# Hybrid attention and MoE layer, one core: the last four experts combined one by one on TensorE's row strips, with the sums and the residual kept in PSUM

## The chip, the cores and the metric

The kernel runs on one core of a Trainium2 chip. The metric is the device time of one execution in microseconds (us), as the median of several runs; lower is better. Engines are named as in the profile: PE is TensorE, PEld its weight loads, DVE VectorE, ACT ScalarE, POOL GpSimd, SP the engine that issues nearly all transfers.

## The reference

One decoder layer on 256 tokens of width 1024, in float32. Two groups of attention heads share one input projection; their outputs go through one output projection and are added to the residual. The part that matters here is the channel mixer behind it, a mixture of 32 experts, of which each token uses two:

```python
def hier_moe(h, ...):                  # h = rms_norm(x): 256 tokens x 1024
    g = argmax(t @ router_group)       # one of 4 groups of experts
    top_v, top_e = top_k(e_logits, 2)  # two of the 8 experts in it
    weight = p_group * softmax(top_v)
    ...
    hid = silu(xc @ w_gate[e]) * (xc @ w_up[e])      # 1024 -> 256
    return hid @ w_down[e]                           # 256 -> 1024
    ...
    y = zeros.at[slot_tok].add(out * slot_w)
x = x + y
```

The weights of each expert are three matrices of 1 MB, and all 32 experts are read in every execution: 96 MB of the 122 MB that are read.

## The kernel before

**Stages.** The first third of the time is attention; the rest is a loop over the experts `e = 1 .. 31` (L854 to L877), in groups of `G = 4`. Each expert has room for `CAP = 32` tokens, so the four experts of a group fill 128 rows. Weights come as units of 1 MB through a ring of buffers (`fill`, L117); SP issues them in the order of `units`: gate and up of an expert, then down of the expert two before it. The last two units are the down weights of experts 30 and 31; the very last one is issued in pieces of columns, `CUTS`.

**One expert.** `half` (L635) multiplies the gathered tokens by gate or up weights: eight matmuls with 32 output rows each, placed side by side in four column strips of the array (`tile_position=(0, q * CAP)`), so that four run at a time. `gate` and `up` copy the result out of PSUM (ScalarE at L650, VectorE at L655). `folded` (L657) transposes it in four pieces on TensorE, then VectorE sums (L663, L665), ScalarE applies silu and VectorE multiplies (L667): the result is `hT`. `down` (L675) multiplies `hT` by the down weights, again in four column strips, and copies the four strips into rows of one tile per group, `oG` (`oL` for the last group), by turns on ScalarE (L686) and VectorE (L688).

**One group.** `weighted` (L616) turns the routing weights of a group into a matrix `pT` (tokens by slots): VectorE multiplies the two 0/1 matrices `P` by the weights `W` into the buffers `Ps`, TensorE transposes them, ScalarE copies. `combine` (L699) then multiplies `pT` by the group's outputs and accumulates over the groups in four PSUM banks `y`. It runs in the third expert of the next group. After the seventh group `combined` adds `y` to the residual `x2` on VectorE (L697).

**The end.** `last` (L706) does the down product of expert 31 in five column slices. For each slice: two matmuls in one column strip (L714), a ScalarE copy (L716), two matmuls with the `pT` of the last group (L726), two VectorE adds to `x2` (L727), an output transfer on SP (L728). `warmed` (L670) runs matmuls on zeros as fillers.

**What sets the order.** `pe` (L632) pins TensorE's instructions to the order of the program. The other engines' queues are ordered by a scheduler. PSUM tiles share eight banks through tags (`lg`, `av`, `pp`, `tr`, two each); a tile waits until the tile before the last with its tag was read.

"Down product of expert 30" in this text is the group of eight matmuls that `down` issues for it; in TensorE's timeline it starts at 328.54.

Of the kernel before, what the change touches and what calls it, by code (L numbers as in the profile page):

```python
# [20 lines left out]
P = 128  # L21
S = 256
# [13 lines left out]
CUTS = (0,256,512,768,896,1024)  # L36
# [14 lines left out]
def hybrid_layer_kernel(ctx: ExitStack, tc: tile.TileContext, x, xt, w_in, w_out, w_gate, w_up, w_down, smalls, relb, out):  # L51
# [65 lines left out]
    def fill(i, limit=len(units)):  # L117
        while len(tiles) < limit:
            j = len(tiles)
            h = home(j)  # L120
            if h not in pools:
                return
            cap = size[h] - (3 if h == "ring" and over_at - RING <= i < over_at else 0)
            if len(used[h]) >= cap and used[h][len(used[h]) - cap] >= i:
                return
            src, k, parts = units[j]
            t = pools[h].tile([P, 2048], F32, name=f"u{j}", tag=h)
            tv = t.rearrange("p (k f) -> p k f", k=k)
            for q in range(parts):
                if j == 0:  # L130
                    ks = slice(q * k // parts, (q + 1) * k // parts)
                    nc.sync.dma_start(tv[:, ks], src[:, ks])
                    xt_load(2, 4) if q == 0 else xt_load(4, 8)
                elif j < len(units) - 1:
                    nc.sync.dma_start(tv, src)
                else:
                    for a, b in zip(CUTS, CUTS[1:]):
                        nc.sync.dma_start(tv[:, :, a:b], src[:, :, a:b])
            tiles.append(t)
            used[h].append(j)  # L140
# [444 lines left out]
    G = 4  # L585
    x2p = x2.rearrange("t c (p k) -> t c k p", k=KC)
# [28 lines left out]

    def weighted(st):  # L616
        g = st["g"]
        pt = ps.tile([P, 512], F32, name="ptr", tag="tr")
# [5 lines left out]
        if g < E // G - 1:  # L624
            st["pT"] = ex.tile([P, S], F32, name="pT", tag="pT")
            st["o"] = ex.tile([P, D], F32, name="oG", tag="oG")
        else:
            t = pools["late"].tile([P, 2048], F32, name="oL", tag="late")
            st["o"], st["pT"] = t[:, :D], t[:, D : D + S]
# [44 lines left out]

    def down(e, st, hT, low):  # L675
        j0 = (e % G) * CAP
        dv = unit(place[e][2], low).rearrange("p (c n) -> p c n", c=2)
        pd = ps.tile([P, 512], F32, name="pd", tag="tr")
        for c in range(2):
            for j in range(4):  # L680
                pe(nc.tensor.matmul(pd[j * 32 : (j + 1) * 32, :256], hT[:, c, :], dv[:, c, j * 256 : (j + 1) * 256],  # L681
                                    start=c == 0, stop=c == 1, tile_position=(0, j * 32)))
        for j in range(4):
            dst = st["o"][j0 : j0 + CAP, j * 256 : (j + 1) * 256]
# [7 lines left out]
    def combined(st, c, nh):  # L692
        pe(nc.tensor.matmul(y[c][nh], st["pT"][:, c * P : (c + 1) * P], st["o"][:, nh * 512 : (nh + 1) * 512],  # L693
                            start=st["g"] == 0, stop=st["g"] == E // G - 2))
        if st["g"] == E // G - 2:
            dst = x2[:, c, nh * 512 : (nh + 1) * 512]
            nc.vector.tensor_tensor(dst, dst, y[c][nh], op=ALU.add)  # L697

    def combine(st):  # L699
        if not y:  # L700
            y.extend([ps.tile([P, 512], F32, name="y", tag=t) for t in ("lg", "av")] for _ in range(NC))
        for c in range(NC):
            for nh in range(2):
                combined(st, c, nh)

    def last(e, st, hT):  # L706
        j0 = (e % G) * CAP
        dv = unit(place[e][2]).rearrange("p (c n) -> p c n", c=2)

        def first(j):  # L710
            pd = ps.tile([P, 512], F32, name="pd", tag="pp")
            a, b = CUTS[j], CUTS[j + 1]
            for c in range(2):
                pe(nc.tensor.matmul(pd[j0 : j0 + CAP, : b - a], hT[:, c, :], dv[:, c, a:b],  # L714
                                    start=c == 0, stop=c == 1, tile_position=(0, j0)))
            nc.scalar.activation(st["o"][j0 : j0 + CAP, a:b], pd[j0 : j0 + CAP, : b - a], AF.Copy)  # L716

        first(0)
        for j in range(len(CUTS) - 1):
            if j < len(CUTS) - 2:  # L720
                first(j + 1)
            cs = slice(CUTS[j], CUTS[j + 1])
            w = CUTS[j + 1] - CUTS[j]
            for c in range(NC):
                py = ps.tile([P, 512], F32, name="py", tag="lg" if c == 0 else "av")
                pe(nc.tensor.matmul(py[:, :w], st["pT"][:, c * P : (c + 1) * P], st["o"][:, cs], start=True, stop=True))  # L726
                nc.vector.tensor_tensor(x2[:, c, cs], x2[:, c, cs], py[:, :w], op=ALU.add)  # L727
            nc.sync.dma_start(out[:, cs].rearrange("(c p) n -> p c n", p=P), x2[:, :, cs])  # L728
# [125 lines left out]
    for e in range(1, E):  # L854
# [13 lines left out]
        if e == E - 1:  # L868
            warmed(2, "lg")
# [4 lines left out]
    hT = folded(t)  # L874
    down(*queue.pop(0), place[E - 1][0])
    warmed(2, "lg")
# [75 lines left out]
```

## Time and profile before

| | us |
|---|---|
| median of three runs (342.51 to 344.88) | 344.61 |
| the profiled execution | 344.07 |
| its span, first to last instruction | 342.2 |

The times in the rows below are those of the profiled execution, counted from the start of its span; its own time is 1.9 us more than the span. The page gives TensorE 314.2 us of busy time, 92% of the span, VectorE 198.9, ScalarE 140.1. Transfers moved 123.17 MB, at 360 GB/s over the span. A busy TensorE in such a page is not one at its peak: records of matmuls that run side by side overlap, and the time of a group is read from where it starts to where the next one starts.

### The profile page before, as it was taken

What the parts mean: (1) busy time and instruction counts of PE and PEld (TensorE: products, weight loads), DVE (VectorE), ACT (ScalarE), POOL (GpSimd) and SP (SyncE); (2) the same over time, 40 slices, a digit from 0 to 9 for tenths busy, and PEclk for the clock granted to TensorE, in tenths of its full rate; (3) what the DMA queues carried; (4) which work ended last, traced back from release to release, by engine and by line L of the source; (5) the groups of instructions that cost most, each with busy time, mean ns of one, the idle gap of its engine ahead of it and who ended that gap; (6) DMA issues with size and microseconds to landing.
All of it is one profiled execution on the core that took longest, in us unless ns stands there. A gap on an engine that the chain in (4) does not pass through costs nothing.

```text
span 342.2 us, 7096 instructions
## 1 busy us (share of the span) xinstructions
PE 314.2 (92%) x2685; PEld 204.8 (60%) x2685; DVE 198.9 (58%) x604; ACT 140.1 (41%) x363; POOL 13.3 (4%) x21
## 2 busy tenths in 40 slices
PE   6999999999999998999999999999678769958875
PEld 2758876788777788575564755646234524724333
DVE  1759758887999657756364563636233521534533
ACT  4775677868786434324222242322112121222221
POOL 1100001000120131000000000000000000000000
PEclk9999999999999999999999999999699988998999
DMA  6999999999625896599999999999999999999953
GB/s 195 398 385 291 389 387 400 412 411 417 215 67 210 313 422 252 205 415 415 417 415 419 415 416 418 416 411 417 417 419 418 416 417 415 411 419 414 410 175 123
DMA packets 31206, 123.17 MB, mean 360 GB/s; under 512 B 2343, under 2 KB 5972, under 8 KB 22980
## 3 DMA queue, kind: packets, MB, share of 16 engines
q1 hardware_dynamic: 30868, 121.70, 90.1%
q0 software_dynamic: 304, 1.02, 0.9%
q8 instruction: 22, 0.36, 0.4%
q14 instruction: 12, 0.10, 0.1%
HBM read 121.64 MB, written 1.07 MB: 359 GB/s over the span
## 4 chain that ended last, share of the span: by engine, by line
PE 63%; DMA 31%; DVE 3%; ACT 1%; issue 0%; SPq 0%; DVEq 0%
PE pp L251 26%; DMA u<-in_w_gate_dram 12%; DMA u<-in_w_down_dram 12%; PE pgu L643 10%; DMA u<-in_w_up_dram 6%; PE pd L681 5%; PE pg L611 4%; PE y L693 3%; PE ptr L660 3%; PE lg L310 2%; DMA u<-in_w_in_dram 2%; PE pt L337 1%; PE pd L714 1%; PE py L726 1%; PE pt L286 1%; PE at L358 1%
## 5 line engine op out<-in xcount | busy, mean ns | idle before, releaser
L643 PE MATMUL pgu<-u,xe 128*32 128x256 f32 x1024 | 71.6, 399 | 10.9 <-ACT oG L686 4.8
L251 PE MATMUL pp<-hi,xh 128*128 128x512 f32 (+1 forms) x132 | 54.1, 411 | 2.4 <-ACT hi L240 2.4
L643 PEld LDWEIGHTS pgu<-u,xe 128*32 128x32 f32 x1024 | 31.1, 112 | 41.2 <-issue 10.9
L251 PE MATMUL pp<-hi,xl 128*128 128x512 f32 (+1 forms) x132 | 52.6, 399 | 0.0
L686 ACT ACTIVATE oG<-pd 32x256 f32<-32x256 f32 x56 | 20.9, 374 | 76.8 <-PE pd L681 63.2
L251 PE MATMUL pp<-lo,xh 128*128 128x512 f32 (+1 forms) x132 | 52.2, 400 | 0.1
L241 DVE TENSOR_TENSOR lo<-u,hi 128x512 fp32r<-128x512 f32 x62 | 43.2, 713 | 13.4 <-ACT hi L240 13.0
L240 ACT ACTIVATE hi<-u 128x512 fp32r<-128x512 f32 x64 | 39.1, 627 | 18.9 <-PE pp L251 13.0
L688 DVE COPY oG<-pd 32x256 f32<-32x256 f32 x56 | 23.7, 423 | 39.5 <-ACT oG L686 37.6
L681 PE MATMUL pd<-u,hT 128*32 128x256 f32 x496 | 34.7, 398 | 8.7 <-DMA u<-in_w_down_dram 7.0
L251 PEld LDWEIGHTS pp<-hi,xh 128*128 128x128 f32 x132 | 25.5, 194 | 9.9 <-ACT hi L240 4.1
L251 PEld LDWEIGHTS pp<-lo,xh 128*128 128x128 f32 x132 | 25.5, 193 | 6.9 <-issue 1.0
L251 PEld LDWEIGHTS pp<-hi,xl 128*128 128x128 f32 x132 | 25.6, 194 | 4.7
L655 DVE COPY u<-pgu 128x256 f32<-128x256 f32 x32 | 13.5, 423 | 24.6 <-PE pgu L643 24.6
L681 PEld LDWEIGHTS pd<-u,hT 128*32 128x32 f32 x496 | 14.8, 112 | 21.2 <-issue 6.7
L611 PEld LDWEIGHTS pg<-Ps,x2q 128*128 128x128 f32 x224 | 25.5, 192 | 2.9 <-DVE gu L663 2.5
L611 PE MATMUL pg<-Ps,x2q 128*128 128x128 f32 x224 | 26.9, 278 | 0.0
L693 PE MATMUL y<-oG,pT 128*128 128x512 f32 x56 | 25.9, 605 | 0.0
L660 PEld LDWEIGHTS ptr<-sm,u 128*128 128x128 f32 x128 | 14.3, 148 | 14.3 <-issue 11.8
L660 PE MATMUL ptr<-sm,u 128*128 128x128 f32 x128 | 22.4, 300 | 0.0
L663 DVE TENSOR_REDUCE gu<-ptr 128x64 f32<-128x256 f32 x32 | 13.6, 425 | 13.2 <-PE ptr L660 12.4
L650 ACT ACTIVATE u<-pgu 128x256 f32<-128x256 f32 x32 | 12.3, 383 | 14.0 <-PE pgu L643 13.4
(155 smaller groups left out, 327.7 us busy)
## 6 DMA issues: line engine op xcount, KB each, us to landing
u<-in_w_gate_dram SPq DMA_DIRECT2D x32, 1024.0 KB, 20.0
u<-in_w_up_dram SPq DMA_DIRECT2D x32, 1024.0 KB, 19.9
u<-in_w_down_dram SPq DMA_DIRECT2D x31, 1024.0 KB, 20.0
u<-in_w_in_dram SPq DMA_DIRECT2D x11, 1024.0 KB, 12.4
u<-in_w_out_dram SPq DMA_DIRECT2D x4, 1024.0 KB, 14.6
u<-in_w_in_dram SPq DMA_DIRECT2D x2, 512.0 KB, 6.1
x<-in_x_dram SPq DMA_DIRECT2D x2, 512.0 KB, 11.1
bias<-rdr SPq DMA_DIRECT2D x3, 256.0 KB, 4.6
```

The lines of the kernel that those rows point to most:

```text
L240: nc.scalar.activation(hi, raw, AF.Copy)
L241: (nc.gpsimd if u * 4 + k in (0,3,) else nc.vector).tensor_tensor(lo, raw, hi.bitcast(F32), op=ALU.subtract)
L251: yield lambda a=a, w=w, kk=kk, i=i: nc.tensor.matmul(pp, a, w[:, cols], start=first and kk == 0 and i == 0, stop=last and kk == len(hls) ...
L611: pe(nc.tensor.matmul(pg[:, j * P : (j + 1) * P], x2q[:, c, q4 * 4 + j, :], st["P"][c][1], start=c == 0, stop=c == NC - 1))
L643: pe(nc.tensor.matmul(pg[q * CAP : (q + 1) * CAP, :HID], st["xe"][:, k, j0 : j0 + CAP], wv[:, k, :], start=r == 0, stop=r == KC // ROWS_Q ...
L655: nc.vector.tensor_copy(t[:, HID : 2 * HID], pg[:, :HID])
L660: pe(nc.tensor.transpose(pt[:, j * P : (j + 1) * P], t[:, j * P : (j + 1) * P], ident))
L663: nc.vector.tensor_reduce(gu[:, :2], parts[:, :2], axis=AX.X, op=ALU.add)
L681: pe(nc.tensor.matmul(pd[j * 32 : (j + 1) * 32, :256], hT[:, c, :], dv[:, c, j * 256 : (j + 1) * 256], start=c == 0, stop=c == 1, tile_pos ...
L686: nc.scalar.activation(dst, pd[j * 32 : (j + 1) * 32, :256], AF.Copy)
L688: nc.vector.tensor_copy(dst, pd[j * 32 : (j + 1) * 32, :256])
L693: pe(nc.tensor.matmul(y[c][nh], st["pT"][:, c * P : (c + 1) * P], st["o"][:, nh * 512 : (nh + 1) * 512], start=st["g"] == 0, stop=st["g"] ...
```

## The change

The last group (experts 28 to 31) is no longer combined as a whole.

- `weighted_last` makes a `pT` for each of its four experts. The expert's 32 weighted columns are repeated four times, so that after the transpose they stand on all four blocks of 32 rows. This is four pairs of VectorE products and transposes, and four ScalarE copies, where there was one of each pair.
- `down` of these experts leaves the result as it lies in PSUM: block `j` of 32 rows holds columns `256 j` to `256 j + 255`. `moved` copies it out, 128 columns by ScalarE and 128 by VectorE, instead of four copies of strips.
- `spread` adds one expert to `y`: for each `j` and each half `c` of the tokens a matmul on the 32 rows of block `j`, in row strip `j` of the array (`tile_position=(j * CAP, 0)`), into bank `y[j]`. The banks are now split by columns (four of 256), with both halves of the tokens in each.
- The residual is added in PSUM too: `residual` multiplies `x2` by the identity, four matmuls of 256 columns for each half of the tokens. The four adds of L697 and the ten of L727 are gone.
- In the last unit (down weights of expert 31) the pieces are now the first 128 of 256 rows whole, then the other 128 in two halves of columns. `last` does the product of the first rows, two fillers, and then each half: product, move, sums, copies from `y` to `x2`, and one output transfer from each of two queues, ScalarE's and SP's.
- In TensorE's order `folded` of expert 31 moves ahead of the down product of expert 29; the residual's matmuls stand behind the down products of 28 and 29, the sums of experts 28 and 29 ahead of the down product of 30.

```diff
-CUTS = (0,256,512,768,896,1024)
+CUTS = ((0, 0, 1024), (1, 0, 512), (1, 512, 1024))
...
+    CROSS = [(j, c) for c in range(NC) for j in range(4)]
...
+    def weighted_last(st):
+        t = pools["late"].tile([P, 2048], F32, name="oL", tag="late")
+        st["o"], st["pT"] = t[:, :D].rearrange("p (i n) -> p i n", i=G), t[:, D:].rearrange("p (i t) -> p i t", i=G)
+        for i in range(G):
+            pt = ps.tile([P, 512], F32, name="ptr", tag="tr")
+            for c in range(NC):
+                q = st["P"][c][1].rearrange("p (j s) -> p j s", j=G)
+                e = st["g"] * G + i
+                nc.vector.tensor_scalar(q, st["P"][c][0][:, i : i + 1, :].broadcast_to([P, G, CAP]),
+                                        W[:, c, e : e + 1], None, op0=ALU.mult)
+                pe(nc.tensor.transpose(pt[:, c * P : (c + 1) * P], q.rearrange("p j s -> p (j s)"), ident))
+            nc.scalar.activation(st["pT"][:, i, :], pt[:, :S], AF.Copy)
...
+    def moved(st, i, pd, rows):
+        nc.scalar.activation(st["o"][rows, i, :P], pd[rows, :P], AF.Copy)
+        nc.vector.tensor_copy(st["o"][rows, i, P:], pd[rows, P:256])
+
+    def spread(st, i, pairs):
+        for j, c in pairs:
+            r = slice(j * CAP, (j + 1) * CAP)
+            pe(nc.tensor.matmul(y[j][:, c * 256 : c * 256 + 256], st["pT"][r, i, c * P : (c + 1) * P],
+                                st["o"][r, i, :], start=False, stop=i == G - 1 and c == NC - 1, tile_position=(j * CAP, 0)))
...
+    def residual(c):
+        for j in range(4):
+            pe(nc.tensor.matmul(y[j][:, c * 256 : c * 256 + 256], ident, x2[:, c, j * 256 : (j + 1) * 256],
+                                start=False, stop=False))
...
     def last(e, st, hT):
...
+        down_product(hT, dv, pd, (0,), range(4))
+        warmed(2, "pp")
+        for nh in range(2):
+            down_product(hT, dv, pd, (1,), (2 * nh, 2 * nh + 1))
+            moved(st, G - 1, pd, slice(nh * 64, nh * 64 + 64))
+            j0 = 2 * nh
+            spread(st, G - 1, [(j, c) for c in range(NC) for j in (j0, j0 + 1)])
+            for c, eng in enumerate((nc.scalar, nc.sync)):
+                for j in (j0, j0 + 1):
+                    dst = x2[:, c, j * 256 : (j + 1) * 256]
+                    if j == j0:
+                        nc.scalar.activation(dst, y[j][:, c * 256 : c * 256 + 256], AF.Copy)
+                    else:
+                        nc.vector.tensor_copy(dst, y[j][:, c * 256 : c * 256 + 256])
+                eng.dma_start(out[c * P : (c + 1) * P, nh * 512 : nh * 512 + 512], x2[:, c, nh * 512 : nh * 512 + 512])
...
         if e == E - 1:
-            warmed(2, "lg")
+            hT = folded(t)
         if e > 1:
             down(*queue.pop(0), place[e][0])
         if e == OVER_E:
             overflow()
-    hT = folded(t)
+        if e == E - 2:
+            residual(0)
+    residual(1)
+    spread(st, 0, CROSS)
+    spread(st, 1, CROSS)
     down(*queue.pop(0), place[E - 1][0])
-    warmed(2, "lg")
+    spread(st, 2, CROSS)
     last(E - 1, st, hT)
```

The order of the built programs shows what this moves. In these rows the names are those of the tiles, `sm` holds the identity, `x_64` is `x2`, numbers belong to units of weights, and brackets name the engines or transfer queues (DMAHW) whose signals an instruction waits for. First, TensorE behind the up product of expert 30. Before:

```order
L623 MATMUL ptr<-sm,Ps 128x128 x2
L681 MATMUL pd<-u_3204,hT 32x256 [waits DMAHW0_49,DVE_49,PE_49]
L681 MATMUL pd<-u_3204,hT 32x256 x7
L643 MATMUL pgu<-u_3206,xe 32x256 [waits DMAHW1_49,Activation_49]
L643 MATMUL pgu<-u_3206,xe 32x256 x7
```

Now:

```order
L627 MATMUL ptr<-sm,Ps 128x128 x2
L627 MATMUL ptr<-sm,Ps 128x128 [waits DVE_49] x2
L627 MATMUL ptr<-sm,Ps 128x128 [waits DVE_49,Activation_49]
L627 MATMUL ptr<-sm,Ps 128x128 [waits DVE_49]
L627 MATMUL ptr<-sm,Ps 128x128 [waits DVE_49,Activation_49]
L627 MATMUL ptr<-sm,Ps 128x128 [waits DVE_49]
L690 MATMUL pd<-u_3224,hT 32x256 [waits DMAHW0_49,Activation_49]
L690 MATMUL pd<-u_3224,hT 32x256 x7
L730 MATMUL y<-x_64,sm 128x256 x4
L655 MATMUL pgu<-u_3226,xe 32x256 [waits DMAHW1_49]
```

One pair of transposes became four, six of them with a wait for VectorE, and four residual matmuls (L730) stand ahead of the gate product of expert 31. VectorE at the same place, before:

```order
L697 TENSOR_TENSOR x_64<-x_64,y 128x512 [waits PE_49,Pool_49]
L655 COPY u_3083<-pgu 128x256 [waits DMAHW6_49,PE_49]
L688 COPY oL<-pd 32x256 [waits Activation_49] x2
L663 TENSOR_REDUCE gu<-ptr 128x64 [waits DVE_49,PE_49]
L665 TENSOR_REDUCE gu<-ptr 128x64
L655 COPY u_3206<-pgu 128x256 [waits DMAHW1_49,PE_49]
```

Now:

```order
L667 COPY u_3103<-pgu 128x256 [waits DMAHW6_49,PE_49]
L625 TENSOR_SCALAR Ps<-Pm,W 128x128 [waits PE_49] x6
L710 COPY oL<-pd 128x128 [waits Activation_49]
L675 TENSOR_REDUCE gu<-ptr 128x64 [waits PE_49]
L677 TENSOR_REDUCE gu<-ptr 128x64
```

The add to the residual is gone, and six products for the new weights stand behind the copy of the up product of expert 30, each with a wait for TensorE.

Second, TensorE between the down products of experts 29 and 30. Before:

```order
L681 MATMUL pd<-u_3258,hT 32x256 [waits DMAHW3_49,DVE_49]
L681 MATMUL pd<-u_3258,hT 32x256 x7
L660 MATMUL ptr<-sm,u_3206 128x128 [waits DVE_49,PE_49,Activation_49]
L660 MATMUL ptr<-sm,u_3206 128x128
L660 MATMUL ptr<-sm,u_3206 128x128 [waits DVE_49]
L660 MATMUL ptr<-sm,u_3206 128x128
L681 MATMUL pd<-u_3260,hT 32x256 [waits DMAHW4_49,DVE_49,PE_49]
L681 MATMUL pd<-u_3260,hT 32x256 x7
```

Now:

```order
L690 MATMUL pd<-u_3282,hT 32x256 [waits DMAHW3_49,PE_49]
L690 MATMUL pd<-u_3282,hT 32x256 x7
L730 MATMUL y<-x_64,sm 128x256 x4
L715 MATMUL y<-oL 128x256 x8
L715 MATMUL y<-oL 128x256 [waits DVE_49]
L715 MATMUL y<-oL 128x256 x7
L690 MATMUL pd<-u_3284,hT 32x256 [waits DMAHW4_49,PE_49]
L690 MATMUL pd<-u_3284,hT 32x256 x7
```

The transposes of expert 31 have left this place, and the second half of the residual and the sums of two experts (L715) have come.

Third, VectorE at the end. Before:

```order
L665 TENSOR_REDUCE gu<-ptr 128x64
L688 COPY oL<-pd 32x256 [waits Activation_49]
L667 TENSOR_TENSOR hT<-gu 128x64 [waits DVE_49,Activation_49]
L688 COPY oL<-pd 32x256 [waits Activation_49] x2
L727 TENSOR_TENSOR x_64<-x_64,py 128x256 [waits PE_49] x6
L727 TENSOR_TENSOR x_64<-x_64,py 128x128 [waits PE_49] x4
```

Now:

```order
L710 COPY oL<-pd 128x128 [waits Activation_49] x2
L710 COPY oL<-pd 64x128 [waits Activation_49]
L749 COPY x_64<-y 128x256 [waits PE_49,Pool_49]
L749 COPY x_64<-y 128x256
L710 COPY oL<-pd 64x128 [waits Activation_49]
L749 COPY x_64<-y 128x256 [waits PE_49,Pool_49]
L749 COPY x_64<-y 128x256 [waits Pool_49]
```

The adds became copies, and the second half's move out of PSUM (the second L710 of 64 rows) stands behind the first half's copies.

## Rows read from the trace of the kernel before

**Rows 1.** Page, part 2: DMA busy share and GB/s in 40 slices.

```profile
DMA  6999999999625896599999999999999999999953
GB/s 195 398 385 291 389 387 400 412 411 417 215 67 210 313 422 252 205 415 415 417 415 419 415 416 418 416 411 417 417 419 418 416 417 415 411 419 414 410 175 123
```

**Rows 2.** Chain that ended last: start us, duration us, what.

```profile
223.82 21.36 DMA u<-in_w_gate_dram
...
305.54 20.03 DMA u<-in_w_down_dram
...
331.99 1.06 PE py L726 x4
...
337.72 0.96 DVE x L727 x4
```

**Rows 3.** Windows at the last weights: busy us by engine, PEclk, DMA share, GB/s.

```profile
327.00:328.00 1.00, 0.36 (x4) 0.12 (x2) 0.73 (x2) 0.52 (x2) 0.00 (x0) 1.00 0.87 288
...
330.00:331.00 1.00, 1.00 (x6) 0.50 (x6) 0.42 (x1) 0.04 (x1) 0.00 (x0) 1.00 0.17 49
```

**Rows 4.** Timeline of TensorE (PE): start us, us, what, [idle before <- its end].

```profile
319.15 0.44 PE L623 MATMUL ptr<-sm,Ps 128*128 128x128 f32 x2
319.52 1.07 PE L681 MATMUL pd<-u,hT 128*32 128x256 f32 x16
320.63 1.07 PE L643 MATMUL pgu<-u,xe 128*32 128x256 f32 x16
...
323.05 1.07 PE L643 MATMUL pgu<-u,xe 128*32 128x256 f32 x16 [0.76 <-DMA u<-in_w_up_dram]
324.06 0.60 PE L673 MATMUL warm<-zeros 128*128 128x512 bf16 x2
325.70 1.07 PE L681 MATMUL pd<-u,hT 128*32 128x256 f32 x16 [1.04 <-DMA u<-in_w_down_dram]
...
328.54 1.07 PE L681 MATMUL pd<-u,hT 128*32 128x256 f32 x16 [1.18 <-DVE gu L665]
```

**Rows 5.** Chain, where TensorE alone sets the pace: start us, us, what.

```profile
177.85 0.86 PE pgu L643 x16
178.71 0.58 PE ptr L660 x4
179.30 1.00 PE pgu L643 x16
```

**Rows 6.** Timeline of VectorE (DVE): the copies of two up products.

```profile
319.29 0.42 DVE L655 COPY u<-pgu 128x256 f32<-128x256 f32 x1 [0.27 <-PE pgu L643]
...
324.19 0.43 DVE L655 COPY u<-pgu 128x256 f32<-128x256 f32 x1 [1.06 <-PE pgu L643]
```

**Rows 7.** Groups by line and shape: busy us, mean ns of one, idle before.

```profile
L595 DVE TENSOR_SCALAR Ps<-Pm,rstd 128x128 f32<-128x128 f32 x16 | 3.9, 279 | 0.0
L623 PE MATMUL ptr<-sm,Ps 128*128 128x128 f32 x16 | 3.5, 300 | 0.0
...
L727 DVE TENSOR_TENSOR x<-x,py 128x128 f32<-128x128 f32 x4 | 1.0, 287 | 0.6 <-PE py L726 0.6
...
L716 ACT ACTIVATE oL<-pd 32x128 f32<-32x128 f32 x2 | 0.5, 269 | 2.6 <-PE pd L714 2.6
```

**Rows 8.** Timeline of TensorE at the attention's products on 64 rows.

```profile
50.69 0.93 PE L310 MATMUL lg<-kT,qT 64*128 64x128 f32 x8
51.55 0.50 PE L251 MATMUL pp<-hi,xh 128*128 128x512 f32 x1
```

**Rows 9.** DMA issues: what, count, KB each, median us to landing.

```profile
out_dram<-x SPq DMA_DIRECT2D x3, 256.0 KB, 2.1
...
out_dram<-x SPq DMA_DIRECT2D x2, 128.0 KB, 1.8
```

**Rows 10.** Windows: granted clock (PEclk, the third column from the end) of one stretch.

```profile
308.00:310.00 2.00, 2.00 (x17) 1.24 (x20) 0.81 (x3) 0.64 (x2) 0.00 (x0) 0.50 1.02 416
```

**Rows 11.** Timeline of TensorE ahead of that stretch.

```profile
306.65 1.35 PE L643 MATMUL pgu<-u,xe 128*32 128x256 f32 x16 [2.45 <-DVEq L733]
```

More of the change, by code (lines that the diff above doesn't have):

```diff
@@ L136, in fill @@
                 else:
-                    for a, b in zip(CUTS, CUTS[1:]):
-                        nc.sync.dma_start(tv[:, :, a:b], src[:, :, a:b])
+                    for c, a, b in CUTS:
+                        nc.sync.dma_start(tv[:, c, a:b], src[:, c, a:b])
             tiles.append(t)
@@ L623, in weighted @@
             pe(nc.tensor.transpose(pt[:, c * P : (c + 1) * P], q.rearrange("p g s -> p (g s)"), ident))
[L624 to L629, printed above, removed]
+        st["pT"] = ex.tile([P, S], F32, name="pT", tag="pT")
+        st["o"] = ex.tile([P, D], F32, name="oG", tag="oG")
         nc.scalar.activation(st["pT"], pt[:, :S], AF.Copy)
@@ L673, in warmed, with down_product @@
             pe(nc.tensor.matmul(t, zeros, zeros.unsqueeze(1).broadcast_to([P, 4, P]), start=True, stop=True))
+    def down_product(hT, dv, pd, cs, js):
+        for c in cs:
+            for j in js:
+                pe(nc.tensor.matmul(pd[j * 32 : (j + 1) * 32, :256], hT[:, c, :], dv[:, c, j * 256 : (j + 1) * 256],
+                                    start=c == 0, stop=c == 1, tile_position=(0, j * 32)))
     def down(e, st, hT, low):
-        j0 = (e % G) * CAP
+        i = e % G
         dv = unit(place[e][2], low).rearrange("p (c n) -> p c n", c=2)
         pd = ps.tile([P, 512], F32, name="pd", tag="tr")
[L679 to L682, printed above, removed]
+        down_product(hT, dv, pd, range(2), range(4))
+        if st["g"] == E // G - 1:
+            moved(st, i, pd, slice(0, P))
+            return
         for j in range(4):
-            dst = st["o"][j0 : j0 + CAP, j * 256 : (j + 1) * 256]
+            dst = st["o"][i * CAP : (i + 1) * CAP, j * 256 : (j + 1) * 256]
             if j % 2 == 0:
@@ L699, in combine @@
+    def spread(st, i, pairs):
[3 more added lines that the diff above has]
+                                st["o"][r, i, :], start=False, stop=i == G - 1 and c == NC - 1, tile_position=(j * CAP, 0)))
+    y = []
     def combine(st):
         if not y:
-            y.extend([ps.tile([P, 512], F32, name="y", tag=t) for t in ("lg", "av")] for _ in range(NC))
+            y.extend(ps.tile([P, 512], F32, name="y", tag=t) for t in ("lg", "lg", "av", "av"))
@@ L702, in combine @@
         for c in range(NC):
-            for nh in range(2):
-                combined(st, c, nh)
+            for j in range(4):
+                pe(nc.tensor.matmul(y[j][:, c * 256 : c * 256 + 256], st["pT"][:, c * P : (c + 1) * P],
+                                    st["o"][:, j * 256 : (j + 1) * 256], start=st["g"] == 0 and c == 0, stop=False))
+    def residual(c):
+        for j in range(4):
+            pe(nc.tensor.matmul(y[j][:, c * 256 : c * 256 + 256], ident, x2[:, c, j * 256 : (j + 1) * 256],
+                                start=False, stop=False))
@@ L706, in last @@
     def last(e, st, hT):
-        j0 = (e % G) * CAP
         dv = unit(place[e][2]).rearrange("p (c n) -> p c n", c=2)
[L710 to L728, printed above, removed]
+        pd = ps.tile([P, 512], F32, name="pd", tag="tr")
```

8 lines of the change are left out of this document (2 added, 6 removed).

## The prediction

> **What bounds the kernel now.** Read the page's slices first [rows 1]: from the 18th slice on the DMA row stands at 9 nearly to the end, at 410 to 419 GB/s. So the weights of the experts stream in without a pause, and the question at the end is who is late: the stream or TensorE. The chain of waits [rows 2] says that five weight transfers, one behind the other, carry the time from 223.82 to 325.57 us (the first and the last are shown); from there it is a chain of TensorE, ScalarE and VectorE work that ends in a VectorE add at 338.68, and 3.5 us later the span ends (the last output transfer and the program's end). The windows of the last weights (four of 1 us, the first and the last in [rows 3]) show the stream falling from 288 GB/s to 49 between 327 and 331, so the last weight is there at about 330.3.
>
> The tail is therefore worth reading instruction by instruction, and the reader should look at TensorE's idle times [rows 4]. From the transposes at 319.15 to the down product of expert 30 at 328.54, TensorE waits 0.76 us for up weights, 1.04 for down weights, and 1.18 for VectorE's sums (a PSUM buffer), and runs a filler pair of 0.6. That is about 3.6 us of room in 9.4 us, and all that the change adds ahead of that down product has to fit in there. TensorE works in the order in which the program is written, so nothing added can step aside.
>
> **The change part by part.** I follow TensorE's clock through the new order. Three prices come from rows. In one mode of the array a matmul with 256 columns in float32 is two records 0.216 us apart: eight such column-tiled matmuls, four at a time, take 0.86 [rows 5]. The same product takes 1.00 after transposes of the full array, and four transposes of 0.11 each take 0.58 after a product; so a change of the array's tiling costs some 0.14. Two full-array matmuls of 256 columns took 1.06 beside column tiles (331.99, [rows 2]): 4 × 0.216 plus 0.20.
>
> Weights of the last four experts. Now one pair of transposes takes 0.37 (319.15 to 319.52, [rows 4]). There will be four pairs, on the same two buffers Ps. VectorE can begin six of the eight products only after its copy of the up sums, which ends at 319.71 [rows 6], and each then waits until TensorE has read the buffer. A round is 0.28 VectorE and a transpose of 0.30 [rows 7], with a hand-over of 0.07 each way (the product that ends at 324.12 is copied from 324.19, [rows 4, 6]): 0.72. From 319.76, two whole rounds and of the third both products and a hand-over (0.28 + 0.28 + 0.07) put the last transpose at 321.83; with its 0.11 and a change of the array the next product starts at 322.04 instead of 319.52: **+2.5 us**. No row shows such a ping-pong. If the waits were free, six more transposes cost 0.7; if the two buffers went strictly in turn, 3 × 0.95 = 2.9. I take 2.5, since the durations in it are all in the trace.
>
> Residual on TensorE. Eight full-array matmuls of 256 columns: 4 × 2 × 0.216 + 0.20 = 1.93 for each half, **3.9 us** in all; without the 0.20 it would be 3.5. What goes for it is VectorE work (four adds beside the combine) on which nobody in the tail waited, so nothing comes back here.
>
> Up to the down product of expert 30: the down product of expert 28 (1.0) and the first residual put the gate of 31 at 324.97 instead of 320.63, so 4.3 us late. The transposes of 30 (0.59) bring its up product to 326.56; before it was 323.05, with its 0.76 of waiting gone, so 3.5 late. The transposes of 31 now come next. Their second pair needs VectorE's copy of the up product, which ended 1.57 us after that product's start (323.05, copy 324.19 + 0.43, [rows 4, 6]), so at 328.13; the down product of 29 follows at 328.45. It was 325.70: 2.8 late, since the filler and the 1.04 of waiting are gone. Then 1.0 for it, 1.93 for the second residual, and the first two of the new single-expert sums. Such a sum is eight matmuls on 32 rows each, four at a time in four row strips of the array. The nearest row is the two-strip product of the attention [rows 8]: eight records of 64 rows took 0.86 from start to the next start; one strip after the other, their columns alone (four records of 256 columns, four of 128) are 1.3. Strips run beside each other, so I take 4 × 0.216 = 0.86 per sum, 1.93 for two with the changes of the array. The down product of 30 then starts at 333.31, not at 328.54: **4.8 us late**, while its weights have been there since about 328. TensorE, not the stream, ends the kernel.
>
> From that down product to the last sum. Before: 328.54 to 338.68, 10.1 us. After: product 1.07; both engines move it out in turn, as one waits for the other on that buffer: 0.27 + 0.29 (ScalarE 128 columns 269 ns, VectorE 287, [rows 7]) and three hand-overs of 0.07; sum of expert 30: 1.0; first half of the last product 0.57; filler 0.53. That is 3.9. Then for the first half: second part of the product 0.6, moves 0.76, sum (four matmuls, two at a time) 1.13, two copies on each engine 0.9 (0.42 each on VectorE, [rows 6]); for the second half the move stands behind those copies in both queues, 0.6 more until TensorE can go, then 1.13 and 0.9. Sum 10.0. The slices of before are gone (five products one after another in a single column strip, ten adds), but the two halves are a longer hand-over: **−0.1 us**.
>
> Output. The last transfer was 128 KB with 1.8 us to landing; one of 256 KB took 2.1 [rows 9]. Now two of 256 KB are issued together from two queues. Between 0.3 (2.1 against 1.8) and 1.0 more (both through one after the other); I take **+0.6**. The two earlier outputs lie under the second half. The ScalarE queue's own issue stands before copies that wait for TensorE anyway; if that cover went, it would be some 0.4.
>
> Last down weight in three pieces. Larger rows should hold the stream's rate, so the 0.77 MB of those four windows would be there at 329 instead of 330.3. Since TensorE comes to this unit at about 336.1, this is worth nothing. In the rest of the program eight matmuls of 256 columns stand for four of 512 in each combine, the same columns; up to 223.82 TensorE is the chain, but then the stream is for the next 90 us [rows 2], which swallows a tenth of a microsecond per group.
>
> Sum: 4.8 − 0.1 + 0.6 = 5.3. On the profiled execution's 344.07: **349.3 us**; that execution lies 0.5 below the median of the three runs, 344.61, so +1.4% on either.
>
> By the Trainium skill, "TensorEngine Tiling (Array Packing)", Key Properties, a change of tiling mode drains TensorE, which speaks against a change that adds a third mode; that page of the skill gives no price, the trace's 0.14 to 0.20 agrees with it, and as I count 17 changes after 319.15 against 16 before, the sum would move by no more than 0.2. By "TensorE: Matmul & The Clock Gate", Measured speedup vs the span model, four row strips gained 3.07 times and not 4; by that a sum of one expert would be an estimated 1.13 us in place of 0.86, and the forecast about 1 us later; no run here shows four strips yet.
>
> **The rivals.** First, *the additions are mostly hidden*: the buffer waits of the new weights are free (0.7 instead of 2.5), the changes of the array cost nothing more (four of 0.2 off), the outputs 0.3. Then 5.3 − 1.8 − 0.8 − 0.3 = 2.4, 346.5 us, within 1%. For it: all three are prices no row of before shows as such. Against it: TensorE's order is fixed, and the matmuls alone exceed the room.
>
> Second, on the other side, *the stream still ends the kernel*: TensorE is never behind, and the end follows the last weight at 329, through the second part of the product, moves, sum, copies (0.6 + 0.8 + 1.1 + 0.9), 0.9 for the first half's copies, and 3.5 + 0.6 to the end: 337.4 of span, 339.3 us. It decides from the point where the added work before the down product of 30 is less than the room of 3.6 us; I count 2.5 + 3.9 + 1.9.
>
> Third, *the four strips run one after the other*: eight matmuls then take 3.46, three full sums cost 2.6 more each and two halves 0.87 each: 9.5 more, 358.8 us. The two-strip row speaks against it.
>
> Granted clock: of two levels, 1.2 and 2.4 GHz, the trace shows the lower one (0.50) at 308 to 310 [rows 10], after TensorE had waited 2.45 us [rows 11]. In the new tail the longest wait is some 1.5; if the clock fell there, the last sum would be 0.9 longer.
>
> **How the numbers follow.** Forecast 0.72, hidden 0.16, stream 0.06, strips in turn 0.06. The bounds of the forecast's own costs reach from 346.5 (all low) to 351.0 (weights 2.9, outputs 1.0, clock 0.9), and the three runs of before differ by 2.4 between themselves. A range of 345.0 to 351.5 leaves out the two small cases and little else. About 1% is what a measurement of this kernel can tell from no change, that is from 341.2 to 348.1. Of the forecast's 0.72 some 0.60 lies above 348.1; with the strips 0.66 for slower. Within 1%: 0.16 + 0.12 = 0.28. Faster: 0.06.
>
> **What would show it.** In the changed profile: the down product of expert 30 at about 333 with no wait for DMA before it; 2.5 us between the first new transpose and the next product; residual groups of 1.9 and sums of 0.9; an end chain of TensorE without weights after 315. I am wrong if TensorE still waits for down weights after 325, or if the gap from that product to the last copy is far from 10.

## The result, and the profile after

The changed kernel takes 348.57 us (median of 5 runs, 347.56 to 351.44), the kernel before, run beside it, 342.78 (5 runs): ratio 1.0154, 95% interval 1.0126 to 1.0182, so 5.3 us more by the ratio (the two medians lie 5.8 apart). The forecast was 5.3.

The profiled execution of the changed kernel (351.44 us, span 349.6) is the longest of its five. It comes to the first new transpose 2.65 us later than that of before (321.80 against 319.15). Part of that is the granted clock (third column from the end), which fell to its lower level ahead of it, after TensorE had waited 1.07 us for down weights (to 311.78) and during a wait of 1.43 for ScalarE (to 314.27). The changed kernel, then the one before:

```profile
314.00:316.00 2.00, 1.73 (x16) 0.68 (x16) 0.43 (x1) 0.14 (x1) 0.00 (x0) 0.51 1.01 412
```

```profile
314.00:316.00 2.00, 2.00 (x12) 1.16 (x9) 1.00 (x3) 0.64 (x2) 0.00 (x0) 1.00 1.02 416
```

Five variants below whose TensorE has the same order up to there (`e1_no_residual`, `e3_half_residual`, `e4_old_pieces`, `e6_whole_last`, `e12_free_buffers`) show a clock of 1.00 in that stretch and come to the transpose at 317.70 to 319.40. So nothing ties this delay to the change, and the two tails are compared from the first new transpose on.

First the page's transfer slices of the changed kernel (busy share, GB/s), to be read against [rows 1]:

```profile
DMA  6999999998536775999999999999999999999603
GB/s 204 400 385 313 387 387 407 412 411 365 181 120 238 318 297 235 334 424 416 416 417 416 412 416 418 415 417 418 412 418 417 416 418 414 414 415 415 255 2 120
```

Before, the last four slices were 414, 410, 175, 123; now the last but one holds 2. For a whole slice of 8.7 us hardly anything is transferred: the weights are there and TensorE is still at work. Its timeline in that stretch (start, us, what, [idle before <- its end]) answers to [rows 4]:

```profile
321.80 0.44 PE L627 MATMUL ptr<-sm,Ps 128*128 128x128 f32 x2
322.61 0.52 PE L627 MATMUL ptr<-sm,Ps 128*128 128x128 f32 x2 [0.37 <-DVE Ps L625]
323.41 0.43 PE L627 MATMUL ptr<-sm,Ps 128*128 128x128 f32 x2 [0.28 <-DVE Ps L625]
324.18 0.43 PE L627 MATMUL ptr<-sm,Ps 128*128 128x128 f32 x2 [0.34 <-DVE Ps L625]
324.54 1.07 PE L690 MATMUL pd<-u,hT 128*32 128x256 f32 x16
325.55 1.99 PE L730 MATMUL y<-x,sm 128*128 128x256 f32 x8
327.47 1.07 PE L655 MATMUL pgu<-u,xe 128*32 128x256 f32 x16
...
331.04 1.07 PE L690 MATMUL pd<-u,hT 128*32 128x256 f32 x16
332.04 1.99 PE L730 MATMUL y<-x,sm 128*128 128x256 f32 x8
333.97 2.01 PE L715 MATMUL y<-oL 32*128 32x256 f32 x32
335.91 1.07 PE L690 MATMUL pd<-u,hT 128*32 128x256 f32 x16
337.70 1.15 PE L715 MATMUL y<-oL 32*128 32x256 f32 x16 [0.72 <-DVE oL L710]
...
341.20 1.13 PE L715 MATMUL y<-oL 32*128 32x256 f32 x8 [0.69 <-DVE oL L710]
342.26 0.62 PE L690 MATMUL pd<-u,hT 128*32 128x256 f32 x4
343.76 1.15 PE L715 MATMUL y<-oL 32*128 32x256 f32 x8 [0.87 <-DVE oL L710]
```

The reader is to see that no wait here is for DMA: the three that [rows 4] show for weights and for sums of VectorE are gone, and those that are left are hand-overs between engines. (The chain of waits, by which the prediction wanted to see this too, reaches back only to 343.38 in this profile.) Read from start to start, the four pairs of transposes take 2.74 us, a residual group 1.92 and 1.93, the sums of two experts 1.94.

VectorE at the end of the same run:

```profile
342.47 0.76 DVE L749 COPY x<-y 128x256 f32<-128x256 f32 x2 [1.33 <-PE y L715]
343.41 0.29 DVE L710 COPY oL<-pd 64x128 f32<-64x128 f32 x1 [0.18 <-ACT oL L709]
345.04 0.76 DVE L749 COPY x<-y 128x256 f32<-128x256 f32 x2 [1.33 <-PE y L715]
```

The second half's move (343.41) stands behind the first half's copies, and TensorE is idle for 0.87 us ahead of the sum that needs it (343.76). The last copy ends at 345.80, 3.8 before the end of the span. The output transfers on the page (KB each, median us to landing), against [rows 9]:

```profile
out_dram<-x ACTq DMA_DIRECT2D x2, 256.0 KB, 2.1
out_dram<-x SPq DMA_DIRECT2D x2, 256.0 KB, 2.4
```

And the windows at the last weights (GB/s last), against [rows 3]:

```profile
326.00:327.00 1.00, 1.00 (x7) 0.87 (x6) 0.28 (x1) 0.00 (x0) 0.00 (x0) 1.00 0.99 387
...
330.00:331.00 1.00, 0.82 (x8) 0.40 (x4) 0.60 (x2) 0.00 (x0) 0.00 (x0) 1.00 0.09 35
```

Between these two it falls over 293, 238 and 199, as it fell before (288 to 49 in four windows): the larger pieces did not hold the stream's rate.

### The profile page after: what moved, and what is told of

It is laid out like the page before. It is cut to its first block, busy times and chain, and to the rows that moved or that the text cites. A ratio compares the mean times of both kernels' runs of the same rounds, so it can differ in the third digit from the quotient of the medians.

```text
span 349.6 us, 7318 instructions
## 1 busy us (share of the span) xinstructions
PE 315.4 (90%) x2801; PEld 217.5 (62%) x2801; DVE 194.6 (56%) x599; ACT 140.2 (40%) x364; POOL 13.4 (4%) x21
## 3 DMA queue, kind: packets, MB, share of 16 engines
HBM read 121.64 MB, written 1.07 MB: 351 GB/s over the span
## 5 line engine op out<-in xcount | busy, mean ns | idle before, releaser
L725 PE MATMUL y<-oG,pT 128*128 128x256 f32 x112 | 25.8, 384 | 0.0
L725 PEld LDWEIGHTS y<-oG,pT 128*128 128x128 f32 x112 | 21.3, 196 | 2.6
```

Source lines behind the costliest of these rows:

```text
L725: pe(nc.tensor.matmul(y[j][:, c * 256 : c * 256 + 256], st["pT"][:, c * P : (c + 1) * P], st["o"][:, j * 256 : (j + 1) * 256], start=st["g ...
```

## The experiments

Theory: TensorE's fixed order ends the kernel, the new work counts in full beyond a room of some 3.6 us ahead of the down product of expert 30, and its place, not its kind, is what costs. Rivals: the end follows the stream, or the costs lie in the buffer waits, the pieces or the outputs. Differences are ratios times the median of before in the same comparison (343.4 to 343.7 us).

**What the parts cost.** `e1_no_residual`: the changed kernel without the residual's matmuls.

```diff
-        if e == E - 2:
-            residual(0)
-    residual(1)
```

> The changed kernel without its sixteen records of residual matmuls; the output lacks the residual. The changed kernel stands 5.3 us above the one before. My theory (TensorE's fixed order ends the kernel, the two residual groups of 1.93 us lie wholly on it): 3.9 us less, so 1.4 us above the kernel before, and the down product of expert 30 starts 10.2 us after the first transpose of the new weights instead of 14.1. Rival (the stream of weights, or the longer hand-overs and outputs after it, end the kernel): no change, 5.3 above. Rival (the residual is half hidden in waits for weights): 2 us less, 3.3 above.

Measured: ratio 1.0017 (0.9996 to 1.0039), +0.6. The first new transpose and the down product of expert 30 in its trace:

```profile
317.70 0.44 PE L627 MATMUL ptr<-sm,Ps 128*128 128x128 f32 x2
...
327.82 1.07 PE L690 MATMUL pd<-u,hT 128*32 128x256 f32 x16
```

The product starts 10.12 us after the transpose, where it was 14.11, and still waits for no transfer. So 3.99 of the lateness is the residual, which is most of the loss. The timed gain is larger than the forecast 3.9: +1.4 was expected, and the upper end of the interval is +1.3.

`e3_half_residual`: only two of the four column blocks go through TensorE, VectorE adds the other two at the end.

```diff
-        for j in range(4):
+        for j in (0, 2):
...
-                        nc.vector.tensor_copy(dst, y[j][:, c * 256 : c * 256 + 256])
+                        nc.vector.tensor_tensor(dst, dst, y[j][:, c * 256 : c * 256 + 256], op=ALU.add)
```

> The changed kernel with the residual through TensorE for the half of the columns that ScalarE copies out, while VectorE adds it to the other half at the end instead of copying (0.42 us each, as a copy). My theory: each residual group falls from 1.93 to 1.07 us, the tail stays 9.9 us: 1.7 us less, 3.6 above the kernel before. Rival (outputs or hand-overs end the kernel): 5.3 above. If the adds at the end cost more than copies, up to 0.3 of the gain is lost.

Measured: 1.0108 (1.0091 to 1.0125), +3.7. Each group takes 1.06 in place of 1.92: half the matmuls, half the columns' time, and the 0.20 beside it stays.

`e2_weights_early`: the new weights in the last group's first expert, ahead of the branch for overflowing experts, where TensorE waits anyway.

```diff
-        if i == 2:
+        if i == (2 if g < E // G - 1 else 0):
```

> The changed kernel with the four pairs of weight products and transposes moved two experts ahead (into expert 28), where the trace of before shows TensorE waiting 1.3 us for down weights and 2.4 at a branch. My theory: they are hidden there, so the 2.7 us that they take behind the up product of expert 30 go: 2.6 us above the kernel before instead of 5.3. The buffer waits stay as they are (the four pairs still take some 2.5 us in their new place). Rival (TensorE's delay at the branch is handed on to the end): 5.3 above as now. Rival (the weights' ping-pong was hidden all along): 5.3 above.

Measured: 1.0067 (1.0042 to 1.0092), +2.3. At the new place the four pairs take longer (3.07 us, 301.66 to 304.73), but the down product behind them waits for nothing there; in the kernel before it waited 1.33 us for its weights (at 303.13).

`e12_free_buffers`: the changed kernel, each product in a buffer of its own.

```diff
-                q = st["P"][c][1].rearrange("p (j s) -> p j s", j=G)
+                q = x2q[:, c, i, :].rearrange("p (j s) -> p j s", j=G)
```

> The changed kernel, but the eight products for the new weights each go to a buffer of their own (the copy x2q of the tokens, which is free by then), so that none waits for a transpose, and VectorE can run them far ahead. My theory: the two buffers are what makes four pairs of transposes take 2.74 us; without them TensorE needs 4 x 0.37 and at most 0.4 of waiting for the two PSUM buffers that ScalarE empties, 1.5 to 1.9, and all behind it comes that much earlier: 0.8 to 1.2 less than the changed kernel, +4.2 against the kernel before (bounds 3.7 to 4.7). Rival, the wait only moves (to ScalarE's copies, or to the next stop in TensorE's order, the up copy of expert 31): no change, +5.0 to +5.3.

Measured: 1.0119 (1.0098 to 1.014), +4.1. TensorE's timeline:

```profile
319.40 0.66 PE L627 MATMUL ptr<-sm,x2q 128*128 128x128 f32 x4
320.31 0.71 PE L627 MATMUL ptr<-sm,x2q 128*128 128x128 f32 x4 [0.26 <-ACT oL L628]
321.22 1.07 PE L690 MATMUL pd<-u,hT 128*32 128x256 f32 x16 [0.20 <-ACT oL L628]
```

1.82 us in place of 2.74; what is left of waiting is for ScalarE's copies. The down product of expert 30 comes 13.18 after the first transpose, 0.93 earlier than with two buffers, so nothing behind it takes the gain back.

**The room.** `e5_dead_residual`: the kernel before, with the residual's eight matmuls at their two places and their results unread.

```diff
+    def dead(c):
+        t = ps.tile([P, 512], F32, name="dead", tag="pp")
+        for j in range(4):
+            pe(nc.tensor.matmul(t[:, :256], ident, x2[:, c, j * 256 : (j + 1) * 256], start=True, stop=True))
...
+        if e == E - 2:
+            dead(0)
+    dead(1)
```

> The kernel before, with eight dead matmuls at the two places of the residual (four against the identity behind the down product of expert 28, four behind that of 29), their result thrown away; all else as before. My theory: the first group of 1.93 us is nearly swallowed by the waits for up weights (0.76), the fillers' stretch (1.04) and 0.1 before expert 31's gate; the second stands ahead of expert 31's transposes and its whole 1.93 reaches the end: 2.0 us above the kernel before. Rival (TensorE alone sets the pace there): 3.9 above. Rival (the stream sets the end): 0.

Measured: 1.0012 (0.9999 to 1.0026), +0.4. The expectation missed. TensorE ahead of the down product of expert 30 (the last row):

```profile
326.85 1.99 PE L709 MATMUL dead<-x,sm 128*128 128x256 f32 x8
328.68 0.60 PE L660 MATMUL ptr<-sm,u 128*128 128x128 f32 x4
329.21 1.07 PE L681 MATMUL pd<-u,hT 128*32 128x256 f32 x16
```

The wait of 1.18 us of [rows 4] is not there: the product starts 0.53 after the transposes of expert 31, while VectorE's sums for them begin only at 329.32. VectorE in this variant:

```profile
328.24 0.43 DVE L688 COPY oL<-pd 32x256 f32<-32x256 f32 x1 [0.44 <-ACT oL L686]
329.32 0.43 DVE L663 TENSOR_REDUCE gu<-ptr 128x64 f32<-128x256 f32 x1 [0.65 <-PE ptr L660]
```

In the kernel before, the same copy, the second one of expert 29's product, stands behind the sums:

```profile
328.02 0.41 DVE L665 TENSOR_REDUCE gu<-ptr 128x64 f32<-128x256 f32 x1
328.47 0.43 DVE L688 COPY oL<-pd 32x256 f32<-32x256 f32 x1
```

So the scheduler gave VectorE another order here. Before, the product starts (328.54) while expert 29's is still being copied; here it starts (329.21) ahead of the sums. So it does not lie in the buffer of expert 29's product there, nor in that of the transposes here: the two kernels have it in different PSUM buffers, and only in the one before does it need the sums (a tile does not always take the buffer of the tile before the last with its tag). Most of the wait before was for weights anyway: those of expert 30 were issued at 308.1 and landed at 328.12, which leaves some 0.4 of the 1.18 to VectorE. So this wait proved to be room too, as the prediction had counted it. Of the two groups' 3.75 us (1.92 and 1.83), 0.52 arrive at that product (9.91 after the transposes at 319.30, before 9.39): the room is 3.2 us.

`e11_dead_double`: the same with eight matmuls at each place.

```diff
-        for j in range(4):
+        for j in (0, 1, 2, 3) * 2:
```

> The kernel before with sixteen matmuls of identity and residual whose results nobody reads, eight behind each of the down products of experts 28 and 29: twice the residual of the changed kernel. The four and four of it gave +0.4 in the kernel before, with no wait left ahead of the down product of expert 30. My theory: the room is used up there, so the second 3.9 us count in full: +4.3 (bounds 3.6 to 4.9). Rival, TensorE's added work stays hidden behind the stream: +0.4 to +1.0.

Measured: 1.0106 (1.0084 to 1.0128), +3.6.

```profile
318.07 0.44 PE L623 MATMUL ptr<-sm,Ps 128*128 128x128 f32 x2
...
319.44 3.72 PE L709 MATMUL dead<-x,sm 128*128 128x256 f32 x16
...
327.22 3.72 PE L709 MATMUL dead<-x,sm 128*128 128x256 f32 x16
...
331.30 1.07 PE L681 MATMUL pd<-u,hT 128*32 128x256 f32 x16
```

The groups take 3.65 and 3.55 to the next start, 7.20 in all. The product of expert 30 is at 13.23 from the first transposes, 3.84 late: a room of 3.4. The second eight matmuls add 3.45 to the groups and not 3.9, and 3.32 of it arrives, so the time lies at the lower bound of what was expected. Work that the kernel has no use for costs just the part that sticks out of the room.

**The pieces.** `e4_old_pieces`: the changed kernel, the last weight in the five pieces of before.

```diff
-                    for c, a, b in CUTS:
-                        nc.sync.dma_start(tv[:, c, a:b], src[:, c, a:b])
+                    for a, b in zip(CUTS, CUTS[1:]):
+                        nc.sync.dma_start(tv[:, :, a:b], src[:, :, a:b])
```

> The changed kernel with the last down weight in the five column pieces of before. My theory: TensorE reaches that weight at about 336, after every piece has landed in either form, so the pieces are worth nothing: +5.3 us against the kernel before, as the changed kernel (bounds 4.7 to 5.9). Rival, the larger pieces hold the stream's rate and that helps: then this kernel is slower than the changed one, +6.6 (1.3 us more, the time between 329 and 330.3). In the windows at the end of the stream I expect the same fall of the rate as with the larger pieces.

Measured: 1.0142 (1.0114 to 1.017), +4.9, not told apart from the changed kernel. Its windows from 326 fall over 313, 248 and 202 to 55 GB/s, as with the larger pieces.

**The place.** `e7_branch_residual_early`: all the work is done, at other places; the branch comes after expert 24 (`OVER_E`), the residual after 25 and 26, the weights as in `e2_weights_early`.

```diff
-OVER_E = 28
+OVER_E = 24
...
-        if e == E - 2:
-            residual(0)
-    residual(1)
+        if OVER_E < e <= OVER_E + NC:
+            residual(e - OVER_E - 1)
```

> The changed kernel, with the added work taken out of the end by its place alone: the weights of the last group at its first expert, the branch for overflowing experts after expert 24 instead of 28, and the two residual groups behind the experts 25 and 26, where TensorE waits for the stream. All work is done. My theory: only the place of the 2.4 and 3.9 us costs, so the down product of expert 30 starts when its weights are there, at 328.2 to 329, and 9.9 to the last copy and 5.7 to the end of the execution give 344.1: +0.3 against the kernel before (bounds -0.5 to +1.2). Rival, the work costs what it costs wherever it stands in TensorE's order: +5.3, or +3 with the weights alone hidden.

Measured: 1.002 (1.0002 to 1.0039), +0.7.

```profile
319.89 1.07 PE L655 MATMUL pgu<-u,xe 128*32 128x256 f32 x16 [0.66 <-DMA u<-in_w_gate_dram]
...
322.38 1.07 PE L655 MATMUL pgu<-u,xe 128*32 128x256 f32 x16 [0.82 <-DMA u<-in_w_up_dram]
...
324.94 1.07 PE L690 MATMUL pd<-u,hT 128*32 128x256 f32 x16 [0.51 <-DMA u<-in_w_down_dram]
...
327.88 1.07 PE L690 MATMUL pd<-u,hT 128*32 128x256 f32 x16
```

TensorE waits for weights again up to the down product of expert 29, so the stream leads up to there and the same matmuls cost nearly nothing.

`e9_before_branch_early`: the kernel before with `OVER_E = 24` alone.

> The kernel before with the branch for overflowing experts after expert 24 instead of 28, nothing else. It asks whether the early branch alone makes a kernel faster, apart from the change. My theory: the end of the kernel before is set by its weights (expert 30's down weights and VectorE's sums let TensorE go on at 328.5), so a TensorE that is early gains at most 0.3: -0.3 (bounds -1.0 to +0.3). Rival, TensorE is late from the branch on, and its 2.4 us and the lower clock behind it come off the end: -2 to -3.

Measured: 1.0 (0.9985 to 1.0015). The early branch by itself is worth nothing in the kernel before. What it gives the changed kernel was not tried apart from the residual's new place.

**The tail behind it.** `e6_whole_last`: the changed kernel, the last expert undivided.

```diff
-        warmed(2, "pp")
-        for nh in range(2):
-            down_product(hT, dv, pd, (1,), (2 * nh, 2 * nh + 1))
-            moved(st, G - 1, pd, slice(nh * 64, nh * 64 + 64))
-            j0 = 2 * nh
-            spread(st, G - 1, [(j, c) for c in range(NC) for j in (j0, j0 + 1)])
+        spread(st, 2, CROSS)
+        down_product(hT, dv, pd, (1,), range(4))
+        moved(st, G - 1, pd, slice(0, P))
+        spread(st, G - 1, CROSS)
```

> The changed kernel, but its last expert goes as a whole: first part of its product ahead of the sum of expert 30 (which waits 0.72 for the move of expert 30 otherwise), no fillers, second part of the product, one move of 128 rows, one sum of sixteen records, eight copies. My theory: the two halves are a longer hand-over, so from the down product of expert 30 to the last copy 6.9 us in place of 9.9 (1.8 for the product and the first part, 1.07 the sum of 30, 0.57, 0.72 the move, 1.07 the sum, 1.7 the copies): 3.0 less, +2.3 against the kernel before (bounds 1.6 to 3.3; at the lower granted clock it would be up to 1 more). Rival, the halves overlap usefully and hide copies and outputs: no gain, +5.3 or more.

Measured: 1.0086 (1.0063 to 1.0109), +3.0. From the down product of expert 30 (332.17) to the last copy (339.14, the end of the chain's last row) it is 7.0, as expected; but from there to the end of the span 4.8 in place of 3.8, which I had left out: the four outputs now go out together, and the page gives the three on SP a median of 2.9 us to landing.

```profile
336.40 1.27 PE y L715 x16
...
337.72 0.42 DVE x L748
...
338.48 0.66 DVE x L748 x2
```

`e8_all`: the placement of `e7_branch_residual_early`, the tail of `e6_whole_last`, and the sum of expert 28 ahead of the transposes of expert 31.

```diff
         if e == E - 1:
+            spread(st, 0, CROSS)
             hT = folded(t)
```

> Both together: work placed early, last expert as a whole; and the sum of expert 28 moved ahead of the transposes of expert 31, where TensorE waits for down weights. My theory: the stream then ends the kernel: last weight at 330.9 to 331.7, second part of the product, move 0.72, sum 1.07, copies 1.7, 3.8 to the end of the span, 1.9 around it: about 341.4, that is -2.1 against the kernel before (bounds -3.5 to -0.8). Rival, the stream's end is not a bound that can be reached, since the pieces come later when TensorE is early or the clock falls in the waits: -0.5 to +0.5.

Measured: 0.9949 (0.9933 to 0.9965), 1.8 us less than the kernel before, near the forecast 2.1. The stream is not the end, though, which the theory took it for: the chain leaves the up weights of expert 31 at 321.76 and is one of engines from there, through

```profile
324.63 1.04 PE pd L690 x16
...
327.50 1.04 PE pd L690 x16
...
330.37 0.61 PE pd L690 x8
```

The three are the down products of experts 29 and 30 and the second part of that of 31, none of which waits for weights.

`e10_moves_first`: as `e8_all`, with two halves again behind the whole product, both moves ahead of both sums.

```diff
-        moved(st, G - 1, pd, slice(0, P))
-        spread(st, G - 1, CROSS)
+        for nh in range(2):
+            moved(st, G - 1, pd, slice(nh * 64, nh * 64 + 64))
+        for nh in range(2):
+            j0 = 2 * nh
+            spread(st, G - 1, [(j, c) for c in range(NC) for j in (j0, j0 + 1)])
```

> As the kernel with all of it, but the last expert in two halves again behind its whole product: both halves' moves first, then the two sums of eight records one behind the other, the copies and outputs of the first half under the second sum. My theory: the last copy comes 0.2 later than with the whole (0.72 + 1.13 + 1.13 + 0.84 + hand-overs in place of 0.72 + 1.15 + 1.75), but 4.8 us from the last copy to the end of the span become 3.8, since half of the output is out by then: 0.75 less than with the whole, -2.5 against the kernel before (bounds -3.2 to -1.6). Rival, the sums of halves cost more than the outputs give back: -1.0 to -1.6.

Measured: 0.9932 (0.991 to 0.9954), 2.3 us less than before, the fastest of all, though not told apart from `e8_all`. The last copy ends 4.2 before the end of the span, between the 3.8 of the halves and the 4.8 of the whole.

## Why the prediction was right

Its steps, counted from the first new transpose in both kernels:

| | predicted | measured |
|---|---|---|
| down product of expert 28 | 2.89 | 2.74 |
| gate of 31 | 5.82 | 5.67 |
| down product of 29 | 9.30 | 9.24 |
| second residual and two sums | 3.86 | 3.87 |
| down product of 30 | 14.16 | 14.11 |
| from there to the last copy | 10.0 | 9.9 |
| last copy to the end, more than before | 0.6 | 0.2 to 0.3 |

**Late at the down product of 30.** 14.11 against 9.39 before is 4.72; the prediction had 4.8. The additions ahead of it are 2.37 + 1.92 + 1.93 + 1.94 = 8.16, so 3.4 of them lay in room. The prediction read 3.6 from TensorE's waits, and the dead matmuls found 3.2 and 3.4. This is the mechanism of the forecast, and the runs bear it out.

**New weights, +2.5.** Measured 2.37 (2.74 less the 0.37 of one pair). Of this, 0.92 is the two buffers, as `e12_free_buffers` shows (1.82 in place of 2.74); the other 1.45 stays with a buffer for each product, 0.46 of it TensorE's waits for ScalarE's copies. A round took 0.80 and 0.77, not 0.72, but VectorE's first product came 0.47 after the first transpose and not 0.61. (The prediction's list of signs has 2.5 for the whole stretch; its sum has 2.89 there, and 2.5 for what is added.)

**Residual, 3.9, nothing back.** 1.92 and 1.93 as forecast, and the kernel without it is 4.0 shorter in the trace. With half of it added by VectorE at the end, the stretch from the down product of expert 30 to the last copy grows from 9.9 to 10.1 only (331.42 to 341.50), and these 0.2 lie in the last sum, whose records took 1.34 instead of 1.15 while the granted clock fell (0.57 at 340.0 to 340.5). The two adds took 0.75 there, the two copies in the changed kernel 0.76: as adds, this half costs nothing more.

**Sums in four row strips.** 1.94 for two, forecast 1.93. The rival with strips in turn asked for 6.9. The Trainium skill, "TensorE: Matmul & The Clock Gate", Measured speedup vs the span model, has 3.07 times for four row strips (at 512 columns), by which two sums would be an estimated 2.3 us; the measurement decides here, and shows them side by side at full rate.

**Tail, −0.1.** 9.9 against 10.1 before. From the end of the first half's copies (343.23) to the second half's sum (343.76) it took 0.53, forecast 0.6; the 0.87 of idle TensorE in the rows begins earlier, under those copies. `e6_whole_last` shows the halves to be a bad bargain in this form: 2.9 us of hand-overs, fillers and order for 1.0 us of outputs. The Trainium skill, "PSUM — Partial Sum Buffer", PSUM bank collisions raise a hardware error, has it that ScalarE and VectorE must not be in the same bank and quadrant at once. The trace agrees in that the program's two moves stand in turn (VectorE's of 343.41 waits for ScalarE's), with 0.72 us of idle TensorE ahead of expert 30's sum; what moves at the same time would do no run here shows.

**Output, +0.6.** The term that was furthest off: 0.2 to 0.3 (3.8 against 3.5 from the last copy to the end of the span), at the low end of its bounds (0.3 and 1.0). The transfers themselves came as forecast: the last one lands at 348.20, 2.4 after the last copy, and before at 340.56, 1.9 after it, so 0.5 more. But the span ends 1.4 after that landing, before 1.7; the prediction had taken this stretch as equal, and why it is shorter stays open.

**Sum.** 4.72 − 0.25 and 0.2 to 0.3 make 4.7 to 4.8 from the traces; the timed difference has an interval of 4.3 to 6.2. So the mechanism was right, but that 5.3 is met to the tenth is luck: the traces speak for some half a microsecond less, within the spread of the runs.

**Pieces of the last weight.** Worth nothing, as priced; but the reason beside it, that larger rows hold the stream's rate, was wrong, and the 0.77 MB were not there at 329. Nothing hung on it.

**Rivals.** Hidden additions (346.5): its low prices were not met for the weights (2.37, and 1.45 even with free buffers, where it had 0.7) nor for the residual (1.92 and 1.93, with the 0.2 beside the columns that it left out); only the outputs came out at its 0.3. Stream as the end: its own condition, additions below the room, is what `e7_branch_residual_early` fulfils, and that kernel lands at +0.7 and not at the rival's 339.3, because the halves' tail and not the last weight follows the down product of 30. The clock did not fall in time to matter: the granted clock is 1.00 from 330 to 344.6, and 0.75 from there to 344.9, where the last sum ends.

## What to carry to other kernels

Where a stream of weights and an engine with a fixed order run side by side, add up that engine's waits ahead of the point where the stream ends: here that much new work was free (3.6 us read, 3.2 to 3.4 measured), and the rest counted in full. The residual's matmuls cost 4 us in the last stage; some 40 us earlier (at 280.9 and 290.2 in `e7_branch_residual_early`) they stand in a kernel that is only 0.7 slower than before with all its additions. So ask first where the operands are ready. Splitting the last step into halves cost more than it gave where the second half's moves queued behind the first half's copies (2.9 us for 1.0 of outputs). With the moves ahead of them it was not told apart from no split, so weigh it against what the outputs give back.

## What was not expected of the hardware

- Four row strips on 32 rows each ran at the full rate: 32 records of 256 columns in 1.94 us (8 × 0.216 = 1.73 at four at a time), changes of the array included.
- Four outputs of 256 KB within a microsecond cost 1.0 us more from the last copy to the end than two at a time (4.8 against 3.8), while two from two queues cost only 0.2 to 0.3 more than one of 128 KB.
- The wait of 1.18 us in [rows 4] vanished when other work stood ahead of it (`e5_dead_residual`), although the sums that the trace names as its end came later than before: a wait's name tells what came last in that run, and most of this one was for weights.
